# A hybrid decoder trunk on one core: the scans' row product gets another step and an explicit place in VectorE's queue

## The chip, the cores and the metric

The kernel runs on one core of one Trainium2 chip. The core has TensorE (PE, the matmuls; its weight loads are shown as PEld), VectorE (DVE), ScalarE (ACT), GpSimd (POOL) and SyncE (SP), which here only issues DMAs. Every engine works through a queue of its own, in order; semaphores tie the queues together. The metric is the device time of one execution in microseconds (us). A profile of one execution gives every instruction's start and length.

## What is computed

One inference step of two layers over 1024 prompt tokens and 8 sequences of 8 new tokens, 1088 columns in all, in fp32, model width 1024. The first layer is a Mamba-2 layer (SSD), the second a pooling layer. The change lies in the scan of the first layer. Per group of heads (8 groups, 4 heads of 64 each) and per chunk of 128 tokens, the reference does this:

```python
y_intra = jnp.einsum('bctsgr,bcsgrp->bctgrp', CB[..., None] * decay, xdt)
decay_end = jnp.exp(acum[:, :, -1:] - acum)
chunk_states = jnp.einsum('bctgn,bctgr,bctgrp->bcgrpn', B, decay_end, xdt)
chunk_decay = jnp.exp(acum[:, :, -1])
def step(h, inp):
    s, d = inp
    return d[..., None, None] * h + s, h
h_final, h_prev = lax.scan(step, h0.reshape(b, G, R, P, N), ...)
y_inter = jnp.einsum('bctgn,bctgr,bcgrpn->bctgrp', C, jnp.exp(acum), h_prev)
y = (y_intra + y_inter).reshape(b, L, H, P)
...
y = (y + d_skip.astype(jnp.float32)[:, None] * xs).reshape(b, L, D_INNER)
gated = (y * jax.nn.silu(z.astype(jnp.float32))).reshape(b, L, N_GROUPS, D_INNER // N_GROUPS)
gated = gated * lax.rsqrt(jnp.mean(gated * gated, axis=-1, keepdims=True) + EPS)
gated = gated.reshape(b, L, D_INNER) * norm_g.astype(jnp.float32)
return gated.astype(h.dtype) @ w_out, new_conv, new_ssm
```

The line before the last two, the product of the gated rows with 1/rms (and with the norm's weight), is what is moved here. It is called the row product below.

## The kernel before

Tokens lie along the columns, channels on the 128 partitions. Large matmuls are done as three passes over a split of the operands into a high and a low part (`mm3`, L190 to L192). The Mamba-2 layer runs the eight groups' scans one after the other, and beside each scan, as filling for TensorE, matmuls of something else: beside groups 0 to 4 the input projection of later groups (`proj_group`), beside groups 4 to 7 the output projection's first parts (`op_units`).

`ssd_layer` writes this interleaving out. A scan is a generator (`scan_group`) of 13 steps. Step 0 loads the first chunks' decays and does `front(0)`, step 1 `front(1)`; steps 2, 4, 6 and 8 do `states` and `rows` for two chunks and one `front`; the odd steps between do one `front`. Then the sample tokens follow. The table `FILL[g]` says how many units of filling go behind each of the first eleven steps. The last two steps of a scan are run later, out of the variable `rest`, while the next group's scan is under way:

- the first (L735 to L745) sums the squares with a matmul, takes 1/rms on ScalarE (L740 and `rstd`, L318), writes it to DRAM (`rsd`, L742) and reads it back, broadcast to all partitions (`rs`, L745). It goes behind the first unit of filling of step 0;
- the second (L748 to L758) is the row product: two VectorE instructions of 128 x 1088 (L749), each followed on SP by the store of its rows to DRAM (`gyd`, L752; not for group 7). Then the slots of `rs` and of the two row tiles are given free. It goes behind the first unit of filling of step 4, or of step 3 for groups 6 and 7. So the row product of group g - 1 is traced in group g's step.

Within a step, `states(c)` computes two chunks' states by matmuls into one PSUM tile (L615) and then the running state: for a group's first chunk a copy (L620), for every other a product on POOL (`hd`, L623) and an addition on VectorE (L624). `rows(c)` computes the two chunks' rows: the part within the chunk (L636), the part from the state (L640), and their eviction on VectorE (L607). `front(c)` transposes (L573, L576), makes the decay mask on ScalarE and VectorE (`M`, L581 to L587), the split operands (`xd`, L589), and ScalarE's copy `Bt` (L593); it also issues the load of a later chunk's decays (`acb`, L549 and L552) on SP.

A unit of `proj_group` ends in ScalarE evictions, and every third unit in a convolution on VectorE (L368 to L372). A unit of `op_units` ends in an eviction on VectorE (`op_evict`, L813, and L816 and L818 for a row's last unit) and hands its last instruction back; a unit of `proj_group` hands back nothing.

The program's order is not yet an engine's order. The instructions are first traced, in the order of the code; then a scheduler fills each engine's queue by its own estimate of when things are ready, and the code's order decides among what is ready. An instruction may so be put ahead of others that were traced before it. `self.tc.issue_after(ins)` is the means against it: whatever is traced inside its block on the engine of `ins` gets an ordering edge, and is queued behind `ins` on that engine. It adds no semaphore.

Of the kernel before, what the change touches and what calls it, by code (L numbers as in the profile page):

```python
# [11 lines left out]
ALU = mybir.AluOpType  # L12
# [87 lines left out]
class Build:  # L100
# [424 lines left out]
    def scan_group(self, g, T):  # L525
        nc, tk, gp, pp = self.nc, self.tk, self.gs, self.pp
# [83 lines left out]
        def states(c, F):  # L610

            S = pp.tile([P, 512], F32, tag="S", bufs=1, name=self.name("S"))
            for i in range(2):
                xde, Bt = F[i][3:5]
                nc.tensor.matmul(S[:, 256 * i:256 * i + 256], Bt, xde.rearrange("p r q -> p (r q)"), start=True, stop=True)  # L615
            for i in range(2):
                cd, Si = F[i][5], S[:, 256 * i:256 * i + 256]
                hn = gp.tile([P, 4, 64], F32, tag="h", bufs=3, name=self.name("h"))
                if h[-1] is None:
                    nc.vector.tensor_copy(hn.rearrange("p r q -> p (r q)"), Si)  # L620
                else:
                    hd = gp.tile([P, 4, 64], F32, tag="hd", bufs=1, name=self.name("hd"))
                    nc.gpsimd.tensor_tensor(out=hd, in0=h[-1], in1=cd.unsqueeze(2).to_broadcast([P, 4, 64]), op=ALU.mult)  # L623
                    nc.vector.tensor_tensor(out=hn, in0=hd, in1=Si.rearrange("p (r q) -> p r q", r=4), op=ALU.add)  # L624
                h.append(hn)

        def rows(c, F):

            py = [pp.tile([P, 512], F32, tag="y", bufs=2, name=self.name("y")) for _ in range(2)]
            for i in range(2):  # L630
                tok, M, xdt, _, _, _, ct = F[i]
                hc, a = h[-3 + i], 128 * i
                for q in range(2):
                    for rr in range(2):
                        r, o = 2 * q + rr, slice(64 * rr, 64 * rr + 64)
                        nc.tensor.matmul(py[q][o, a:a + 128], xdt[:, r, :], M[:, r, :], start=True, stop=(hc is None))  # L636
                    if hc is not None:
                        for rr in range(2):
                            r, o = 2 * q + rr, slice(64 * rr, 64 * rr + 64)
                            nc.tensor.matmul(py[q][o, a:a + 128], hc[:, r, :], ct[:, r, :], start=False, stop=True)  # L640
            for q in range(2):
                evac_y(py[q], q, slice(128 * c, 128 * c + 256), 256)
# [62 lines left out]
        for c in range(0, 8, 2):  # L705
            states(c, F)
            if c == 6:
                load_z()
            Fn = [front(c + 2)]
            if c == 6:  # L710
                self.slots.free(B)
            rows(c, F)
            F = Fn
            if c == 6:
                zsc = sample_inter()
                self.slots.free(C)
            yield
            if c < 6:
                F.append(front(c + 3))
                if c == 4:  # L720
                    load_h0()
                yield
# [813 lines left out]
    def ssd_layer(self):  # L1536
        nc, sl = self.nc, self.slots
        T, rest = {0: self.G[0]["out"]}, iter(())
        self.x = [None] * 8
        self.acts = [[] for _ in PARTS]  # L1540
        self.prep = self.op_part_load(0, self.acts[0])
        self.fill = self.beside(T)
        for g in range(8):
            sc = self.scan_group(g, T[g])
            for i, n in enumerate(FILL[g]):
                next(sc)
                for j in range(n):
                    next(self.fill)
                    if i in (0, 3 + (g < 6)) and j == 0:
                        next(rest, None)  # L1550
                if i == 8 and g + 1 in self.G:
                    T[g + 1] = [sl.get("xbc") for _ in range(4)]
                    for t, d in zip(T[g + 1], self.xbd[g + 1]):
                        nc.sync.dma_start(t, d)
            rest = sc
        self.prep = self.op_part_load(3, self.acts[3])
        self.out_unit()
        next(rest)
        for _ in range(2):
            next(self.fill)  # L1560
        self.out_unit()
        for _ in rest:
            pass
# [331 lines left out]
```

## Time and profile before

| | us |
|---|---|
| three runs | 1605.86, 1607.51, 1612.53 |
| median | 1607.51 |
| profiled execution | 1606.84 |
| its span | 1605.1 |
| mean granted clock of TensorE | 0.997 |

In the profile, a row of the timeline is: start, duration, engine, line, operation, result and operands by their names in the program, shapes, count; in brackets the time that the engine stood idle ahead of it and what ended that. A row of the waits is: who waited, for whom, us in total, how often, the longest. The lines are those of the kernel before. The scans lie between about 340 and 930 us; before them comes the input projection for the first groups, after them the rest of the output projection and the pooling layer. Starts in the chain of waits and in the timeline are from the span's start.

### The profile page before, as it was taken

The page shows a single profiled execution, that of the slowest core. Times are in us where ns is not written, and L with a number is a line of the kernel's source. Part 1 is how long each engine was busy: PE and PEld are TensorE (multiplying, and loading weights), DVE is VectorE, ACT ScalarE, POOL GpSimd, SP SyncE. Part 2 cuts the span into 40 slices and gives each one's busy share as a digit, 9 for nine tenths or more (in the row PEclk, how much of TensorE's full clock was granted, in tenths as well). Part 3 has the DMA queues.
Part 4 walks back from the last instruction along what each step waited for, and adds up shares of the span by engine and source line. Part 5 has one row for each costly group of instructions (what it writes and reads, how often), then busy time and mean ns, then how long its engine had stood idle before and what let it go on. Part 6 is the DMA issues. An engine that isn't in the chain of part 4 may idle for free.

```text
span 1605.1 us, 30689 instructions
## 1 busy us (share of the span) xinstructions
PE 1579.7 (98%) x11946; PEld 1506.9 (94%) x11946; DVE 1292.1 (80%) x2152; ACT 789.5 (49%) x1512; POOL 515.3 (32%) x558
## 2 busy tenths in 40 slices
PE   9999999999999999999999999999999999999997
PEld 7899999998888888888899899999999999999997
DVE  6875879778788888888888867998889867677886
ACT  6663344456666766675545437632322233333364
POOL 0133456512231313130212232265666640000241
PEclk9999999999999999999999999999999999999999
DMA  9423232355555554678998542133323379565783
GB/s 352 166 100 110 69 111 91 102 186 158 187 161 171 156 177 150 214 252 292 303 338 296 206 135 86 53 134 114 115 102 104 111 233 373 152 172 178 161 173 121
DMA packets 122306, 275.58 MB, mean 172 GB/s; under 512 B 18193, under 2 KB 59313, under 8 KB 122161
## 3 DMA queue, kind: packets, MB, share of 16 engines
q1 hardware_dynamic: 118128, 260.90, 47.7%
q0 software_dynamic: 4032, 12.72, 4.7%
q8 instruction: 94, 1.54, 0.4%
q14 instruction: 52, 0.42, 0.1%
HBM read 201.12 MB, written 70.23 MB: 169 GB/s over the span
## 4 chain that ended last, share of the span: by engine, by line
PE 81%; DVE 7%; DMA 5%; issue 4%; ACT 2%; POOL 1%; SPq 0%; DVEq 0%; ACTq 0%; POOLq 0%
PE st L1042 10%; PE st L1040 10%; PE st L1041 10%; PE mm L190 10%; PE mm L191 9%; PE mm L192 9%; PE op L1259 2%; PE op L1260 2%; PE op L1258 2%; PE y L636 2%; PE y L640 2%; DMA rsd<-z 2%; PE S L615 2%; DMA rs<-rsd 1%; PE am L261 1%
## 5 line engine op out<-in xcount | busy, mean ns | idle before, releaser
L1040 PE MATMUL st<-hh,w 128*128 128x272 f32 x832 | 240.2, 289 | 1.0 <-ACT w L182 1.0
L1042 PE MATMUL st<-hh,w 128*128 128x272 f32 x832 | 240.4, 289 | 0.4 <-DVE w L184 0.4
L1041 PE MATMUL st<-hl,w 128*128 128x272 f32 x832 | 240.0, 288 | 0.0
L1040 PE MATMUL st<-t,w 128*128 128x272 f32 x624 | 179.6, 288 | 0.0
L1042 PE MATMUL st<-t,w 128*128 128x272 f32 x624 | 179.5, 288 | 0.0
L1041 PE MATMUL st<-t,w 128*128 128x272 f32 x624 | 179.2, 287 | 0.0
L190 PE MATMUL mm<-hh,wh 128*128 128x368 f32 (+1 forms) x528 | 178.6, 338 | 0.0
L191 PE MATMUL mm<-hl,wh 128*128 128x368 f32 (+1 forms) x528 | 173.1, 328 | 0.0
L192 PE MATMUL mm<-hh,wl 128*128 128x368 f32 (+1 forms) x528 | 172.9, 327 | 0.0
L1040 PEld LDWEIGHTS st<-hh,w 128*128 128x128 f32 x832 | 156.8, 188 | 1.4 <-ACT w L182 1.4
L1042 PEld LDWEIGHTS st<-hh,w 128*128 128x128 f32 x832 | 156.4, 188 | 0.9 <-DVE w L184 0.9
L1041 PEld LDWEIGHTS st<-hl,w 128*128 128x128 f32 x832 | 156.7, 188 | 0.0
L623 POOL TENSOR_TENSOR hd<-h,cd 128x256 f32<-128x256 f32 x56 | 46.9, 838 | 313.3 <-DVE h L624 154.6
L182 ACT ACTIVATE w<-wr 128x512 fp32r<-128x512 f32 x104 | 64.9, 629 | 166.4 <-PE st L1042 135.0
L1259 PE MATMUL op<-b,w 128*128 128x272 f32 x448 | 128.9, 288 | 0.7 <-DVE b L1188 0.7
L1258 PE MATMUL op<-b,w 128*128 128x272 f32 x448 | 129.4, 289 | 0.0
L1260 PE MATMUL op<-b,w 128*128 128x272 f32 x448 | 128.9, 288 | 0.0
L190 PE MATMUL mm<-gh,wh 128*128 128x368 f32 (+1 forms) x372 | 126.0, 339 | 0.2
L192 PE MATMUL mm<-gh,wl 128*128 128x368 f32 (+1 forms) x372 | 122.1, 328 | 0.0
L191 PE MATMUL mm<-gl,wh 128*128 128x368 f32 (+1 forms) x372 | 121.8, 327 | 0.1
L1040 PEld LDWEIGHTS st<-t,w 128*128 128x128 f32 x624 | 117.7, 189 | 0.1
L1042 PEld LDWEIGHTS st<-t,w 128*128 128x128 f32 x624 | 117.4, 188 | 0.0
(307 smaller groups left out, 4572.7 us busy)
## 6 DMA issues: line engine op xcount, KB each, us to landing
wr<-win SPq DMA_DIRECT2D x48, 512.0 KB, 3.8
acb<-acd SPq DMA_DIRECT2D x64, 256.0 KB, 4.2
wr<-pin SPq DMA_DIRECT2D x32, 512.0 KB, 3.7
wr<-pout SPq DMA_DIRECT2D x28, 512.0 KB, 4.9
x<-x1d SPq DMA_DIRECT2D x24, 544.0 KB, 5.8
x1d<-x SPq DMA_DIRECT2D x22, 544.0 KB, 4.5
wr<-pout POOLq DMA_DIRECT2D x20, 512.0 KB, 6.6
x<-xT SPq DMA_DIRECT2D x16, 544.0 KB, 6.8
```

The costliest lines, as they stand in the source:

```text
L182: self.nc.scalar.activation(hi, src, AF.Copy)
L190: nc.tensor.matmul(ps[:, :n], hi[:, k, :], ah[:, a:a + n], start=first, stop=False)
L191: nc.tensor.matmul(ps[:, :n], hi[:, k, :], al[:, a:a + n], start=False, stop=False)
L192: nc.tensor.matmul(ps[:, :n], lo[:, k, :], ah[:, a:a + n], start=False, stop=last)
L615: nc.tensor.matmul(S[:, 256 * i:256 * i + 256], Bt, xde.rearrange("p r q -> p (r q)"), start=True, stop=True)
L623: nc.gpsimd.tensor_tensor(out=hd, in0=h[-1], in1=cd.unsqueeze(2).to_broadcast([P, 4, 64]), op=ALU.mult)
L1040: nc.tensor.matmul(ps[c][:, :QUART], hi[:, k], xh[:, t], start=(k == 0), stop=False)
L1041: nc.tensor.matmul(ps[c][:, :QUART], hi[:, k], xl[:, t], start=False, stop=False)
L1042: nc.tensor.matmul(ps[c][:, :QUART], lo[:, k], xh[:, t], start=False, stop=(k == 3))
L1258: nc.tensor.matmul(ps[:, :QUART], hi[:, k], xh, start=k == 0, stop=False)
L1259: nc.tensor.matmul(ps[:, :QUART], hi[:, k], xl, start=False, stop=False)
L1260: nc.tensor.matmul(ps[:, :QUART], lo[:, k], xh, start=False, stop=k == 7)
```

## The change

The row product's step is traced in step 3 for every group, where groups 1 to 5 had it in step 4. Around it stand two ordering edges: to `self.hins`, which `states` sets to its last update of the state (L620 or L624; in step 3 this is the second update of the group's first two chunks), and, where the unit of filling just run hands back an instruction (groups 5 to 7), to that instruction, the unit's last eviction. Both are on VectorE, so the edges concern the two instructions of L749. The first step of `rest` stays where it was, without an edge.

```diff
                 if h[-1] is None:
-                    nc.vector.tensor_copy(hn.rearrange("p r q -> p (r q)"), Si)
+                    ins = nc.vector.tensor_copy(hn.rearrange("p r q -> p (r q)"), Si)
                 else:
...
-                    nc.vector.tensor_tensor(out=hn, in0=hd, in1=Si.rearrange("p (r q) -> p r q", r=4), op=ALU.add)
+                    ins = nc.vector.tensor_tensor(out=hn, in0=hd, in1=Si.rearrange("p (r q) -> p r q", r=4), op=ALU.add)
                 h.append(hn)
+            self.hins = ins.ins
...
                 for j in range(n):
-                    next(self.fill)
-                    if i in (0, 3 + (g < 6)) and j == 0:
+                    ins = next(self.fill)
+                    if i == 0 and j == 0:
                         next(rest, None)
+                    elif i == 3 and j == 0:
+                        with self.tc.issue_after(self.hins), self.tc.issue_after(ins.ins) if ins else contextlib.nullcontext():
+                            next(rest, None)
```

## The prediction

> **What bounds the kernel now.** I read the page first, for the share of each engine.
>
> ```profile
> PE 1579.7 (98%) x11946; PEld 1506.9 (94%) x11946; DVE 1292.1 (80%) x2152; ACT 789.5 (49%) x1512; POOL 515.3 (32%) x558
> ```
>
> TensorE is busy for 98% of the span, so an edit of VectorE's queue can only gain where TensorE waits. Next I read the waits of TensorE between 340 and 960 us, the part of the span that holds the scans (columns: us in total, times, longest).
>
> ```profile
> PE y L640 <- DVE h L620: 4.1, 4, 1.2
> PE S L615 <- ACT Bt L593: 2.2, 2, 1.4
> PE mm L796 <- ACT raw L434: 2.0, 1, 2.0
> PE y L636 <- DVE M L587: 1.5, 1, 1.5
> ```
>
> The waits of TensorE there add up to 4.1 + 2.2 + 2.0 + 1.5 = 9.8 us (one more, of 0.3, is left out). The largest is that of the inter-chunk row matmul (L640) for the first copy of the state (L620), four times, about 1 us each. Why the copy is late shows in the answer for the row product's line (L749): until what VectorE stood idle ahead of it, in us and times. The chain of waits (start, duration, what) adds where that DMA comes from.
>
> ```profile
>   DMA rs<-rsd: 9.9, 6
> ```
>
> ```profile
> 428.49 5.61 DMA rsd<-z
> 434.12 3.84 DMA rs<-rsd
> ...
> 449.97 0.59 PE y L640 x8
> ...
> 661.20 1.35 DVE xbc L749
> ```
>
> The product of the group before stands ahead of the copy in VectorE's queue, and waits there until the broadcast of 1/rms has come back from DRAM. VectorE stands still for 9.9 us in six such waits, though only four of them reach TensorE. The chain holds such a product four times, first at 437.99 and last at 661.20, so these are groups 1 to 4 (the copy of the group that runs, behind the product of the one before).
>
> **Groups 1 to 4: the wait that goes.** VectorE in the second group (start, duration, line; in brackets the idle time and what ended it), and the state's matmul that the copy needs:
>
> ```profile
> 437.99 1.35 DVE L749 SCALAR_TENSOR_TENSOR xbc<-xbc,vec,rs 128x1088 f32<-128x1088 f32 x1 [2.16 <-DMA rs<-rsd]
> 439.25 0.42 DVE L620 COPY h<-S 128x256 f32<-128x256 f32 x1
> ...
> 448.87 0.41 DVE L624 TENSOR_TENSOR h<-hd,S 128x256 f32<-128x256 f32 x1
> ...
> 454.33 1.34 DVE L749 SCALAR_TENSOR_TENSOR xbc<-xbc,vec,rs 128x1088 f32<-128x1088 f32 x1
> ```
>
> ```profile
> 435.82 0.70 PE L615 MATMUL S<-xd,Bt 128*128 128x256 f32 x2
> ...
> 439.73 0.66 PE L640 MATMUL y<-ea,h 128*64 128x128 f32 x8 [1.19 <-DVE h L620]
> ```
>
> The edge to the state's last update puts both products behind the copy. VectorE is free from 437.99 - 2.16 = 435.83 on and the state's matmul ends at 435.82 + 0.70 = 436.52, so the copy moves from 439.25 to about 436.5, 2.7 us earlier. The row matmul could have begun at 439.73 - 1.19 = 438.54, and the copy is done by then (436.94), with 1.6 us to spare. That takes away 1.19 us here and 4.1 us in the four groups. The broadcast lands at 437.96 and no longer blocks anything, since the next thing that VectorE does is the copy.
>
> By the Trainium skill, "Perfetto Trace Analysis", section "Identifying the Most-Contended Engine", the busy share of matmuls is a poor measure of the headroom and that of the weight loads a better one. The trace has this row for the weight loads:
>
> ```profile
> PEld y L640 <- DVE h L620: 4.9, 4, 1.4
> ```
>
> By it the sum below would come out 4.9 - 4.1 = 0.8 us lower. The trace before doesn't say which of the two rows counts; the rest of this text goes by the matmuls.
>
> **What the products cost where they go.** Nothing is added or dropped: 16 products of 1.35 us, as before, and no DMA more. In groups 1 to 4 the step moves from 4 to 3. The trace tells where that puts them: the second product, traced in step 4, now runs at 454.33, behind that step's updates; so products traced in step 3 will run ahead of step 4's first update (now at 448.87), both of them, 1.35 + 1.34 = 2.69 us. From the copy to that update VectorE has 448.87 - 439.25 = 9.62 us. With the copy at 436.52 the update comes at 436.52 + 9.62 + 2.69 = 448.83 and ends at 449.25. Its reader is the row matmul at 449.97, which by then has moved to 449.97 - 1.19 = 448.78: a new wait of 0.47 us, four times 1.9 us. If one of the products or none falls ahead of the update, this is nothing; that is the lower bound, and I take the upper, because of the row at 454.33. The 2.7 us that the copy gains can be lost on the way too, where its followers wait for TensorE or ScalarE, which don't move with it: then the wait is up to 2.69 us in each group, which is the slower rival below.
>
> **The stores behind the product.** SP's queue is in order too. Two of its rows, one of ScalarE's, and the page's row for the loads (size, us from issue to landing):
>
> ```profile
> 439.36 0.32 SPq L752 DMA_DIRECT2D gyd<-xbc  x1
> 439.78 5.33 SPq L549 DMA_DIRECT2D acb<-acd  x2
> ```
>
> ```profile
> 447.97 1.27 ACT L581 ACTIVATE M<-acb,tka 128x128 f32<-128x128 f32 x4
> ```
>
> ```profile
> acb<-acd SPq DMA_DIRECT2D x64, 256.0 KB, 4.2
> ```
>
> The store of the product (L752) waits on SP for the product, and the load of a chunk's decays stands right behind it. If that order stays and the first product runs at about 444, the load starts some 5 us later. It takes 4.2 us, so it lands now at 444.0 and would land at about 449. By the count of its tiles its reader is the last instruction of the row at 447.97 (about 448.9). So this is covered to within a few tenths; without the cover ScalarE would stand still for up to 5 us in each of four groups. I take 0.
>
> **Groups 5 to 7: the edge to the eviction.** Here the fill is the output projection and both products must also follow one eviction (L818 or L813). For groups 5 and 6 these are the eviction and the next update on VectorE and the update's reader on TensorE:
>
> ```profile
> 750.04 0.22 DVE L818 TENSOR_TENSOR x<-x,gs 128x64 f32<-128x64 f32 x1
> ...
> 752.81 0.42 DVE L624 TENSOR_TENSOR h<-hd,S 128x256 f32<-128x256 f32 x1 [0.49 <-issue]
> 754.07 0.66 PE L640 MATMUL y<-ea,h 128*64 128x128 f32 x8
> ```
>
> ```profile
> 818.66 0.22 DVE L818 TENSOR_TENSOR x<-x,gs 128x64 f32<-128x64 f32 x1
> ...
> 819.61 0.42 DVE L624 TENSOR_TENSOR h<-hd,S 128x256 f32<-128x256 f32 x1 [0.21 <-issue]
> 821.13 0.39 PE L640 MATMUL y<-ea,h 128*64 128x128 f32 x4
> ```
>
> In group 5 the update ends at 753.23, 0.84 us before its reader; in group 6 at 820.03, 1.10 us before it. Both products move from ahead of the eviction to behind it, so VectorE reaches the eviction up to 2.69 us earlier and spends these 2.69 us after it: nothing if the eviction can follow, at most 2.69 - 0.84 = 1.85 and 2.69 - 1.10 = 1.59 us if it can't. I take 0 for both: VectorE shows no idle time ahead of either eviction, so the eviction was waiting for VectorE and can come earlier.
>
> Group 7, VectorE and then TensorE:
>
> ```profile
> 879.28 1.35 DVE L749 SCALAR_TENSOR_TENSOR xbc<-xbc,vec,rs 128x1088 f32<-128x1088 f32 x1 [1.46 <-DMA rs<-rsd]
> ...
> 884.28 0.59 DVE L813 SCALAR_TENSOR_TENSOR x<-mm,gat,x 128x368 f32<-128x368 f32 x1
> ```
>
> ```profile
> 884.19 0.70 PE L615 MATMUL S<-xd,Bt 128*128 128x256 f32 x2 [1.36 <-ACT Bt L593]
> ...
> 886.52 0.44 PE L640 MATMUL y<-ea,h 128*64 128x128 f32 x4
> ```
>
> Here VectorE's wait (1.46) and the first product are what make the split operands of chunk 3 late, and with them ScalarE's copy Bt and TensorE's 1.36 us. With both products behind 884.28 that wait goes: -1.36. VectorE reaches the eviction up to 1.46 + 1.35 = 2.81 us earlier, and not before TensorE has done the unit, whose last matmul stands just ahead of the state's (884.19 - 1.36 = 882.83). I put it at 882.5 to 882.8, estimated from that row; with its 0.59, the products' 2.69 and the update's 0.42 the update ends at about 886.3; its reader moves to 886.52 - 1.36 = 885.16 and waits about 1.0 us. Net about -0.4, between -1.4 (no new wait) and 0.
>
> **The sum.** -4.1 + 1.9 - 0.4 = -2.6 us, between -4.1 - 1.4 = -5.5 and -4.1 + 1.9 + 1.85 + 1.59 = +1.2. The profiled execution took 1606.84 (span 1605.1), so it would take 1604.2. The median of the three runs shown, 1607.51, is 0.67 above it; from there it is 1604.9, which is my forecast. Its own range is 1602 to 1608.7.
>
> **Rivals.**
>
> The next wait takes its place, nothing is gained. The copy is early, but the row matmul's other inputs or the POOL product between the updates end last instead. Against it: the 1.6 us to spare. For it: the updates behind the copy still need POOL's product (hd) between them. About 1607.
>
> More goes than the four waits. VectorE's 9.9 us of standing still are out of the queue; if its lead also covers ScalarE's Bt copies and the masks (2.2 and 1.5 us of TensorE's waits) and the hand-over of group 4 (2.0), 9.8 us go: 1607.51 - 9.8 = 1597.7. Against it: only the 4.1 and 1.36 stand directly behind a product.
>
> Slower: two products in a row become the bound. They are one block of 2.69 us behind the update, on an engine that is busy for 80% of the span. If nothing covers the block, the next mask, split or update is 2.69 us late in seven groups: 18.8 us, less the 5.5 that go, +13.3: 1620.8. It turns slower from 5.5 / 7 = 0.8 us uncovered per group, and by over 0.5% from about 1.9. Against it: before, VectorE carried the same block in two pieces. For it: in groups 5 to 7 the eviction's edge forbids the gaps that were used.
>
> The change doing nothing is excluded for groups 1 to 4, where a product stands ahead of the copy; in groups 6 and 7 both already stand behind the updates, and only the eviction's edge acts.
>
> **How the numbers follow.** Forecast 0.48, nothing gained 0.12, more goes 0.22, slower 0.18. Something over 0.5%, 8.0 us, is about what a measurement of this kernel can tell from no change. The first two cases lie within it: 0.60. The third is faster, 0.22, and the fourth slower, 0.18. The range runs from 1596 (all waits gone, and the 1.6 us by which the lowest run shown lies under the median) to 1613 (the slower case half covered: halfway between 1604.9 and 1620.8).
>
> **What would show it.** After: no wait of L640 for L620, and L749 without idle time before it in groups 1 to 4; L620 within some tenths of the end of its state's matmul (L615); both products between L620 and the next L624; new waits of L640 for L624 of about half a us; S waiting for Bt no longer in group 7. I am wrong if L749 still waits for its DMA, if the waits of L640 for L624 exceed 1 us per group, if M or xd become releasers of TensorE, or if loads of acb show up as releasers of ScalarE.

## The result, and the profile after

| | before | changed kernel |
|---|---|---|
| median of 6 runs, us | 1607.8 | 1602.82 |
| lowest to highest | 1605.86 to 1612.53 | 1600.84 to 1603.68 |
| profiled execution | 1606.84 | 1600.84 |
| its span | 1605.1 | 1599.0 |

The ratio is 0.997, with a 95% interval from 0.9956 to 0.9983: 2.7 to 7.1 us less than before, and no change by the bound of 0.5%. Run again beside the kernels of the experiments (a0 below), the same program gave 0.9987 [0.9979, 0.9996], or 0.6 to 3.4 us less. The two intervals share 2.7 to 3.4 us. The changed kernel's median is the same both times (1602.82 and 1602.94); it is the kernel before that came out slower in its six runs here (1607.8) than in 110 later ones on four chips (medians 1605.94 to 1606.45). So the gain is about 3 us rather than 5.

The kernel's file has one line more from L620 on, so what was L640 is L641 now, L749 is L750, and L813 is L814. The page's row of busy times:

```profile
PE 1579.0 (99%) x11946; PEld 1505.4 (94%) x11946; DVE 1293.0 (81%) x2152; ACT 789.9 (49%) x1512; POOL 515.6 (32%) x558
```

The engines do the same work as before; TensorE's 1579 us now fill a span that is 6 us shorter. TensorE's waits between 340 and 960 us (total, times, longest):

```profile
PE mm L797 <- ACT raw L434: 1.3, 1, 1.3
PE mm L190 <- DVE x L814: 1.1, 1, 1.1
PE y L641 <- DVE h L624: 0.5, 1, 0.5
PE y L637 <- DVE M L587: 0.5, 1, 0.5
...
PE S L615 <- ACT Bt L593: 0.2, 1, 0.2
...
```

The row that led the list before, 4.1 us of the row matmul waiting for the copy of the state (L620), is gone. So is the row of 2.2 us of S waiting for Bt, but for 0.2. Two waits are new: 1.1 us of a filling matmul for an eviction of the output projection (L814), and 0.5 us of the row matmul for an update of the state (L624), in group 6. Three rows of 0.2 to 0.3 us are left out. And what the row product's own line says:

```profile
L750 DVE SCALAR_TENSOR_TENSOR xbc<-xbc,vec,rs x16: 1344/1347/1355, 442.9 to 924.6; 128x1088 f32<-128x1088 f32 x16
its engine sat idle before it (us, times) until:
```

Nothing stands below the heading of the idle time, where 9.9 us for the broadcast of 1/rms stood. VectorE in the second group, and then TensorE there:

```profile
435.87 0.42 DVE L620 COPY h<-S 128x256 f32<-128x256 f32 x1 [0.33 <-PE S L615]
...
442.94 1.35 DVE L750 SCALAR_TENSOR_TENSOR xbc<-xbc,vec,rs 128x1088 f32<-128x1088 f32 x1
...
445.49 1.35 DVE L750 SCALAR_TENSOR_TENSOR xbc<-xbc,vec,rs 128x1088 f32<-128x1088 f32 x1
...
448.04 0.42 DVE L624 TENSOR_TENSOR h<-hd,S 128x256 f32<-128x256 f32 x1
```

```profile
435.13 0.70 PE L615 MATMUL S<-xd,Bt 128*128 128x256 f32 x2
...
436.92 0.66 PE L641 MATMUL y<-ea,h 128*64 128x128 f32 x8
...
449.35 0.66 PE L641 MATMUL y<-ea,h 128*64 128x128 f32 x8
```

The copy follows its matmul at once, and its reader runs without a wait. Both products stand ahead of step 4's first update. But that update's reader (449.35) doesn't wait either, 0.9 us after the update's end.

Where the 6 us went is read by stretches, cut at the starts of a group's first gated row on VectorE (L733, now L734): from group 0's to group 3's, to group 4's, and to group 7's. Before and after (stretch, length, busy time of each engine, granted clock, DMA):

```profile
420.40:643.64 223.24, 220.33 (x1710) 196.87 (x1709) 187.91 (x287) 144.74 (x327) 55.00 (x93) 1.00 0.53 170
643.64:723.27 79.63, 76.43 (x571) 69.40 (x571) 66.69 (x100) 54.77 (x116) 19.52 (x33) 0.98 0.71 231
723.27:917.86 194.59, 191.93 (x1474) 175.56 (x1473) 170.80 (x328) 99.12 (x235) 40.33 (x46) 1.00 0.84 289
```

```profile
419.75:639.41 219.66, 219.66 (x1709) 197.05 (x1708) 188.11 (x286) 144.93 (x327) 56.76 (x93) 1.00 0.54 173
639.41:717.61 78.20, 76.71 (x581) 69.29 (x580) 66.40 (x100) 54.44 (x116) 21.43 (x33) 1.00 0.71 236
717.61:911.41 193.80, 191.78 (x1465) 174.25 (x1464) 171.30 (x328) 99.58 (x235) 39.93 (x46) 1.00 0.83 290
```

In the first stretch, which holds the second to fourth groups' scans, TensorE is now busy for 219.66 of 219.66 us, and 223.24 - 219.66 = 3.58 us are gone. In the next, group 4 and its hand-over to the output projection, 1.43 are gone, and in groups 5 to 7 0.79. That is 5.8 us; the first stretch begins 0.65 us earlier in this execution, which isn't the change's doing (in a0 it begins at 420.57).

Not all of the 5.8 us is the change's doing either. The second stretch before has a granted clock of 0.98. At its end, from 719.2 us on, TensorE ran at half its clock for about 3 us, with its matmuls 0.31 us apart and not 0.167. A window of the kernel before (columns as above), and two of its matmuls:

```profile
720.00:722.00 2.00, 2.00 (x10) 2.00 (x8) 2.00 (x2) 1.84 (x4) 1.18 (x2) 0.50 1.00 384
```

```profile
720.43 0.51 PE L796 MATMUL mm<-gh,wh 128*128 128x368 f32 x1
720.73 0.51 PE L797 MATMUL mm<-gh,wl 128*128 128x368 f32 x1
```

By the clock of such windows this dip is worth some 1.7 us, an estimate. The changed kernel's stretches have none, in this execution and in a0. In a0 the three stretches are 3.52, 0.46 and 0.62 us shorter than before. So the first stretch is what both executions show; with the dip taken off, the other two together lie between 0.5 us less and 0.6 us more than before.

### The profile page after: what moved, and what is told of

It reads as the page before. It is cut to its first block, busy times and chain, and to the rows that moved or that the text cites. A ratio compares the mean times of both kernels' runs of the same rounds, so it can differ in the third digit from the quotient of the medians.

```text
span 1599.0 us, 30692 instructions
## 1 busy us (share of the span) xinstructions
PE 1579.0 (99%) x11946; PEld 1505.4 (94%) x11946; DVE 1293.0 (81%) x2152; ACT 789.9 (49%) x1512; POOL 515.6 (32%) x558
```

## The experiments

The theory after the result: (1) the gain is the product at the head of VectorE's queue, which waited for 1/rms and held the copy back; (2) the ordering edge removes it, not the step; (3) the new wait of 1.9 us that the prediction counted fell away because TensorE's queue was sorted anew too. The rivals: the step does it, groups 5 to 7 do it, or the products never come near the reader. Each kernel below keeps the line numbers of before (L749, L640, L813), and its time stands beside the kernel before on the same chip. Medians are of 9 to 12 runs each.

**e2 and e1: the step alone, and the edge to the state's update.** Against the kernel before; e2 has the first change of this diff alone, e1 has the edge too (to `self.hins`, set in `states` as in the changed kernel):

```diff
-                    if i in (0, 3 + (g < 6)) and j == 0:
+                    if i in (0, 3) and j == 0:
-                        next(rest, None)
+                        with self.tc.issue_after(self.hins) if i else contextlib.nullcontext(): next(rest, None)
```

> The row product is traced in step 3 for every group, but without either ordering edge. Theory (what counts is that the first product, which waits for its DMA, no longer stands ahead of the state's copy): without the edge the scheduler puts the first product ahead of the copy again, L640 still waits for L620 four times, about 4 us in all, and the time is that of the kernel before within 2 us (ratio 0.999 to 1.001). Rival (the earlier step alone sorts the queues better): the waits of L640 for L620 are gone and the ratio is about 0.997.

> As the changed kernel, but with the edge to the state's update alone, none to the eviction. Groups 1 to 4 are as in the changed kernel. Theory: the gain of groups 1 to 4 stays (4 to 5 us), group 7 keeps its wait for the DMA in front of the product and TensorE its wait of S for Bt (1.4 us), while the new wait of 1.1 us of TensorE for an eviction in group 5 goes: ratio 0.997 to 0.998. Rival (the eviction's edge carries a part of the gain in groups 5 to 7): 2 us or more slower than the changed kernel, ratio 0.9985 or more.

e2: 1605.27 us, ratio 0.9995 [0.9983, 1.0007]. TensorE's wait between 340 and 960 us, and from the product's line the idle time ahead of it:

```profile
PE y L640 <- DVE h L620: 3.1, 5, 1.2
```

```profile
  DMA rs<-rsd: 9.9, 6
```

e1: 1603.49 us, ratio 0.9983 [0.9974, 0.9992]. Its waits show no L640 for L620; S waits for Bt as before:

```profile
PE S L615 <- ACT Bt L593: 2.2, 3, 0.9
```

```profile
  DMA rs<-rsd: 0.9, 1
```

Without an edge the product is back at the queue's head, with all of its 9.9 us, although it was traced a step earlier: the step alone doesn't take that wait away, and the time can't be told from that of before. It isn't without effect on TensorE, though: up to group 3's first gated row the waits for the copy fall from 2.9 to 1.5 us and the stretch from 223.24 to 221.56 us, while group 5 has a wait of 1.2 us that it didn't have. With the edge no wait for the copy is left in groups 1 to 4, and the stretch is 219.70 us (e1); with the old step and the edges it is 220.18 (e3 below). Most of it is the edge. e1's ratio lies just above the range expected, which held 4 to 5 us.

**e4 and e5: which groups.** e4 has the change for groups 1 to 4, e5 for groups 5 to 7; the other groups are as before.

> The change for groups 1 to 4 alone; groups 5 to 7 have the step and the order of the kernel before. Theory: nearly all of the gain is here, 4 to 5 us, ratio 0.997 to 0.9975; L640 no longer waits for L620. Rival (groups 5 to 7 give a good part): a gain of 2.5 us or less, ratio 0.9985 or more.

> The change for groups 5 to 7 alone; groups 1 to 4 have the step and the order of the kernel before. Theory: the wait of S for Bt in group 7 goes (1.4 us), a wait for an eviction in group 5 comes (1.1 us), the four waits of L640 for L620 stay: within 1.5 us of the kernel before, ratio 0.999 to 1.001. Rival (these groups give a good part): a gain of 2.5 us or more, ratio 0.9985 or less.

e4: 1603.39 us, ratio 0.9979 [0.997, 0.9988]. e5: 1607.45 us, ratio 1.0003 [0.9993, 1.0013], with four waits of L640 for L620 left (2.7 us). The change in groups 1 to 4 gives about 3 us, less than the 4 to 5 expected; alone in groups 5 to 7 it gives nothing that can be told from zero.

**a0: the changed kernel once more**, with the line numbers of before.

> The changed kernel again, with the line numbers of before, beside the kernels it is to be compared with. All theories: about 1603 us, ratio 0.996 to 0.998 to the kernel before; TensorE shows no wait of the step-4 reader (L640) for the state's copy (L620) in any group, and the row product (L749) no idle time before it.

1602.94 us, ratio 0.9987 [0.9979, 0.9996]; the kernel before took 1605.98 on this chip. The ratio lies just above the range expected, the waits are as expected. Its first stretch:

```profile
420.57:640.29 219.72, 219.72 (x1710) 197.17 (x1708) 187.62 (x286) 144.85 (x327) 56.62 (x93) 1.00 0.53 173
```

219.72 against 219.66: the period of a group is 73.2 us in both executions.

**e7: the reader held in its place.** In TensorE's queue, the reader of step 4's first update stood behind 12 matmuls of filling before the change. In the changed kernel it stands behind 20, some 0.167 us each (counted in TensorE's timeline of the second group, from the L636 ahead of them on). e7 is the changed kernel with edges on TensorE that keep all but 12 of them behind that reader, by putting the unit's later matmuls (`k > 3`), the small matmuls (L261) traced behind the unit, and step 5's `front` and unit behind it (the diff shows a part of this):

```diff
-                            nc.tensor.matmul(py[q][o, a:a + 128], hc[:, r, :], ct[:, r, :], start=False, stop=True)
+                            self.yins = nc.tensor.matmul(py[q][o, a:a + 128], hc[:, r, :], ct[:, r, :], start=False, stop=True)
...
-            self.mm1(ps, w, k, act, ch, k == 0, k == len(acts) - 1)
+            with self.tc.issue_after(self.pin.ins) if self.pin and k > 3 else contextlib.nullcontext(): self.mm1(ps, w, k, act, ch, k == 0, k == len(acts) - 1)
...
-                next(sc)
+                with self.tc.issue_after(self.yins.ins) if i == 5 and 0 < g < 5 else contextlib.nullcontext(): next(sc)
```

> The changed kernel, with edges on TensorE in groups 1 to 4 so that step 4's first reader of the state (L640) stands behind 12 matmuls of filling, as before the change, and not behind 20. Theory A (the prediction's term of 1.9 us was right for a queue of TensorE that stays as it was, and fell away because it was sorted anew): four waits of L640 for L624 of about 0.45 us each, 1.5 to 2.5 us in all, and 1604 to 1606 us, some 1 to 2 us above the changed kernel. Rival B (the products never reach the reader wherever it stands): no such wait, and the time of the changed kernel within 0.7 us. Rival C (a wait appears and is absorbed later, since the scan's eight matmuls have filling behind them that isn't tied to them): the waits as in A, the time as in B.

1606.43 us, ratio 1.0 [0.999, 1.001], beside a0's 0.9987: 0.0013, or 2.1 us, and 3.5 us by the medians. TensorE's waits from the first gated row of group 0 (419.84) to that of group 4 (720.4), and one of the readers:

```profile
PE y L640 <- DVE h L624: 1.7, 4, 0.4
```

```profile
448.64 0.66 PE L640 MATMUL y<-ea,h 128*64 128x128 f32 x8 [0.44 <-DVE h L624]
```

Four waits of about 0.44 us, where the prediction had 0.47. The first stretch shows that they aren't absorbed later:

```profile
419.84:641.53 221.69, 220.39 (x1710) 197.15 (x1709) 187.89 (x286) 144.94 (x327) 56.70 (x93) 1.00 0.54 172
```

221.69 - 219.72 = 1.97 us in three groups, 0.66 in each. Theory A holds: the new wait is there as soon as the reader is left where it was. With it nothing is left of the gain, since the ratio is 1.0; the median lies 0.4 us above theory A's range. What the rival C had for it, filling that isn't tied to the reader, doesn't help an engine that works its queue in order and has no gap later on.

**e3, e9 and e10: both edges, with the step of before.** In a0's form only the step's number differs: 4 for groups 1 to 5 (e3), for groups 1 to 4 (e9), for group 5 (e10).

```diff
-                    if i in (0, 3) and j == 0:
+                    if i in (0, 3 + (g < 6)) and j == 0:
```

> Both edges (behind the state's update and behind the last eviction), but the product traced in step 4 for groups 1 to 5 as before. Theory A (the place in VectorE's queue alone is what counts, and the edges alone set it): the same as the changed kernel, 1602 to 1604 us, no wait of L640 for L620 and no idle time before L749. Theory B (the step counts as well, because a step brings its own units of filling): the products come behind step 4's first update, step 5's update waits for them instead, and the time lies at 1604 to 1607 us.

e3: 1607.28 us, ratio 1.0011 [1.0003, 1.002]: 4.3 us above a0 and slower than the kernel before, and yet without one wait of L640 for L620 and with no idle time ahead of L749. Theory A of this run falls, and so does B: no update waits, and the group's period is 73.36 us, 0.14 above a0's. What is lost, is lost in group 7, and the two halves show from where:

> Both edges everywhere, the product traced in step 4 in groups 1 to 4 only. In the run with the old step everywhere, a group's period was 73.36 us against 73.22 in the changed kernel, and group 7's time between the gated rows of chunk pairs (L733) 60.7 against 54.2. Theory A (in groups 1 to 4 the step hardly counts, since the edge sets the queue's order; the loss of 4 us comes from group 5's step alone, whose store moves the loads of the decays for group 7): 1603 to 1604 us, the period 73.36 us, at most 0.6 us above the changed kernel. Rival B (the step counts in groups 1 to 4 too, in some way that the periods don't show): 1605 us or more.

> Both edges everywhere, the product traced in step 4 in group 5 only. Theory A: three loads of decays (acb) of group 7 issued some 12 us later on SP (at about 863 rather than 851), ScalarE behind, TensorE waiting for the copy Bt about 2 us in group 7, and 1606 to 1608 us, about 4 us above the changed kernel. Rival B: the changed kernel's time within 1 us.

e9: 1602.35 us, ratio 0.9976 [0.9967, 0.9986]. e10: 1607.01 us, ratio 1.001 [1.0001, 1.0019]. The stretch between the first gated rows of groups 6 and 7, of a0 and then of e10:

```profile
859.22:913.43 54.21, 54.15 (x426) 49.14 (x425) 48.80 (x99) 29.63 (x74) 12.78 (x16) 1.00 0.73 260
```

```profile
857.21:917.93 60.72, 57.95 (x431) 49.85 (x430) 49.64 (x99) 31.81 (x82) 13.57 (x16) 1.00 0.74 247
```

It is 6.5 us longer, while the stretch of groups 5 and 6 is 1.4 us shorter. The matmuls (first column) stand still in it for 60.72 - 57.95 = 2.8 us rather than for nothing, the weight loads (second) for 60.72 - 49.85 = 10.9 rather than 54.21 - 49.14 = 5.1. So 5.8 of the 6.5 us show as missing weight loads, and only half of that as idle matmuls. The trace points to SP's queue, of a0 and then of e10:

```profile
850.79 1.85 SPq L549 DMA_DIRECT2D acb<-acd  x3
```

```profile
860.85 0.32 SPq L1627 DMA_DIRECT2D x1d<-x  x1
861.22 2.48 SPq L549 DMA_DIRECT2D acb<-acd  x3
```

Three loads of group 7's decays are queued behind a store that waits for an eviction until 860.85. ScalarE in e10, which has its masks to make from them:

```profile
862.24 0.28 ACT L593 ACTIVATE Bt<-tr 128x128 f32<-128x128 f32 x1 [4.83 <-DVE xd L589]
...
866.79 1.28 ACT L581 ACTIVATE M<-acb,tka 128x128 f32<-128x128 f32 x4 [2.01 <-DMA acb<-acd]
```

In a0 ScalarE made these masks from 856.11 on. In e10 it does so 10.7 us later and is behind from there on; TensorE then waits for Bt:

```profile
PE S L615 <- ACT Bt L593: 2.4, 3, 1.6
```

So in groups 1 to 4 the step makes no difference that can be told, and in group 5 it decides over some 4 us, which are lost two groups later. That the loads of the decays are the cause is read from the trace; moving them alone, and why the queues are sorted so, wasn't tried.

**e6: the product ahead of the copy, with and without its wait.** Both kernels put both products of groups 1 to 4 ahead of the copy (behind the mask of chunk 1, L587, in step 1). In the second, the rows of groups 0 to 3 are multiplied by themselves and not by 1/rms, which leaves the normalisation of these groups out and takes the wait for the reload away. The orders of VectorE's and TensorE's queues are the same in both.

```diff
-                                           in1=rst,
+                                           in1=rst if g > 3 else xs[q],
```

> For groups 1 to 4 the row product is traced in step 1, so that both products stand ahead of the state's copy (L620) in VectorE's queue; the queue's head then waits for the reload of 1/rms with the copy behind it. Theory A (what costs is a product at the head of the queue whose row is still under way, with the copy behind it): the copy comes about 4 us later than in the changed kernel, TensorE's reader L640 waits about 2 to 3 us for it in each of four groups, 1607 to 1613 us, 4 to 10 us above its twin without the reload. Rival B (the products' own busy time ahead of the copy costs, not the wait for the reload): both twins the same within 1 us, and both above the changed kernel by 3 us or more. Rival C (the place in the queue costs nothing): both at 1602 to 1604 us.

> As its twin, but for groups 0 to 3 the rows are multiplied by themselves rather than by the reloaded 1/rms, which leaves the normalisation of these groups out and takes the wait for the reload away; the queues of VectorE and TensorE are the same in both. Theory A: the two products run at once, the copy comes about 2.7 us after the point at which the first could start, TensorE's reader L640 waits 0 to 0.5 us for it, 1602 to 1605 us. Rival B: the time of its twin within 1 us.

With the reload: 1607.76 us, ratio 1.0012 [1.0003, 1.002]; without: 1605.12 us, ratio 1.0 [0.9989, 1.0011]. TensorE's waits between 340 and 960 us of the first, and VectorE at its second group; then VectorE of the second kernel at the same place:

```profile
PE y L640 <- DVE h L620: 3.7, 4, 1.8
```

```profile
437.81 2.61 DVE L749 SCALAR_TENSOR_TENSOR xbc<-xbc,vec,rs 128x1088 f32<-128x1088 f32 x2 [1.78 <-DMA rs<-rsd]
440.34 0.42 DVE L620 COPY h<-S 128x256 f32<-128x256 f32 x1
```

```profile
438.28 2.61 DVE L749 SCALAR_TENSOR_TENSOR xbc<-xbc,vec 128x1088 f32<-128x1088 f32 x2
440.81 0.42 DVE L620 COPY h<-S 128x256 f32<-128x256 f32 x1
```

In the second the wait of L640 for L620 is gone altogether. So with the same queues the reload at their head costs 2.6 us by the medians, and 3.7 us show as TensorE's waits: theory A in kind. Its size was off, 3.7 us rather than 8 to 12; the copy's reader too was queued later, behind 11 matmuls of filling. Rival B holds in part: without the wait the time is still that of the kernel before (ratio 1.0), 1.7 us above e4 (on another chip), whose groups 5 to 7 are as here. From group 0's first gated row to group 3's the two take 223.14 and 220.72 us, and e4 219.71. So of 3.4 us lost there, 2.4 go with the wait and 1.0 with the place of the products ahead of the copy. That 1.0 us shows in no wait of TensorE's matmuls, and where it arises is open.

**e8: groups 5 and 6 as before**, the change for groups 1 to 4 and 7.

> The change for groups 1 to 4 and 7; groups 5 and 6 as before. Theory A (the change's gain lies in the queue-head wait of groups 1 to 4 and in group 7's wait for Bt, and group 5 lost about 1.1 us to an eviction that comes late for a feed-forward matmul): 0.5 to 1.5 us under the changed kernel, 1601.5 to 1602.5 us, a wait of L640 for L620 of about 1.0 us once (group 5), no wait of S for Bt in group 7. Rival B (groups 5 and 6 are a wash, the one wait traded for the other): the changed kernel's time within 0.5 us.

1602.85 us, ratio 0.9982 [0.9973, 0.999], as a0 within the intervals. The new wait for the eviction was gone but for 0.2 us, group 5 had a wait of 0.8 for the copy (before, it had none), and in group 7 S waited for Bt again, in another chunk:

```profile
889.37 0.70 PE L615 MATMUL S<-xd,Bt 128*128 128x256 f32 x2 [1.59 <-ACT Bt L593]
```

Rival B holds. None of these versions can be told from the changed kernel to its advantage; e9's median is the lowest, by 0.6 us on another chip than a0's.

## Why the prediction came out as it did

The forecast was 1604.9 us and 2.6 us of gain; measured were 1602.8 and 5.0, and 2 to 3 us in the repeat. The time lies in the range and within 0.5% of before, as the likeliest case had it. That 2.6 lies so near the repeat is luck in part: without the term that failed the sum would have been -4.5, and waits that it took at nothing came up in groups 5 and 6. By its steps:

- **The wait that goes, -4.1: right.** The copy was put at the end of its matmul; that ends at 435.13 + 0.70 = 435.83, and the copy came at 435.87. No such wait is left, and e2 against e1 shows that the edge does it. The size was rather above: three groups' periods lost 3.58 us, where the rows of the matmuls had 1.2 + 0.8 + 0.9 = 2.9 for these groups. The weight loads' rows had 1.4 + 1.0 + 1.1 = 3.5. In e7 likewise: 1.97 us in three groups, by the matmuls' rows 1.3, by those of the weight loads 2.2. The rule of the Trainium skill, "Perfetto Trace Analysis", section "Identifying the Most-Contended Engine", that the prediction set beside its sum, speaks of busy shares and not of single waits. Carried over to waits, as the prediction did, it agrees with these traces better than the matmuls' rows do: its 0.8 us belonged into the sum.
- **The new wait in groups 1 to 4, +1.9: the step that failed**, at the words "its reader is the row matmul at 449.97, which by then has moved to 449.97 - 1.19 = 448.78". VectorE's side of it was exact: the update was put at 448.83, and came at 448.04 in an execution whose group began 0.65 to 0.7 us earlier. The reader was not left where it was: with 20 matmuls of filling ahead of it, not 12, it came at 449.35, and the prediction's place for it in this execution would have been about 448.1. That is the 8 x 0.167 = 1.3 us more. e7 puts it back, and the wait of 0.44 us appears four times. The term was right for an unchanged queue of TensorE; the change re-sorted that queue as well. (449.97 is the reader's start in the chain. The timeline has it at 449.90, and by it the term is 0.54 us for each group.)
- **Group 7, -1.4 + 1.0: half right.** The eviction and the products follow each other as put, and S waits no more. The new wait didn't come; by the rows the reader stands later here too, though no run held this one in its place. VectorE and then TensorE in group 7:

```profile
878.20 0.60 DVE L814 SCALAR_TENSOR_TENSOR x<-mm,gat,x 128x368 f32<-128x368 f32 x1
878.72 2.60 DVE L750 SCALAR_TENSOR_TENSOR xbc<-xbc,vec,rs 128x1088 f32<-128x1088 f32 x2
881.24 0.42 DVE L624 TENSOR_TENSOR h<-hd,S 128x256 f32<-128x256 f32 x1
```

```profile
878.00 1.02 PE L615 MATMUL S<-xd,Bt 128*128 128x256 f32 x4
...
881.97 0.66 PE L641 MATMUL y<-ea,h 128*64 128x128 f32 x8
```

  The update ends 881.66 - 878.00 = 3.66 us after S begins (put at 886.3 - 882.83 = 3.5), the reader runs 3.97 us after it and not 2.33. Alone, without the changed groups before, it is worth nothing that can be told (e5), and in e8 its wait came back elsewhere.
- **Groups 5 and 6, taken at 0: too little, but within the bounds.** Group 6 has a wait of 0.5 us for the update (0.8 in a0), where the bound was 1.59. At the end of group 5 there is one for an eviction, which the prediction did not have. The changed kernel, and then e1, which lacks only the edge to the eviction:

```profile
790.49 0.43 PE L190 MATMUL mm<-gh,wh 128*128 128x368 f32 x1 [1.06 <-DVE x L814]
```

```profile
792.58 0.43 PE L190 MATMUL mm<-gh,wh 128*128 128x368 f32 x1 [0.22 <-DVE x L813]
```

  At this place it is 0.7 to 1.1 us in all seven versions that have the edge to the eviction in groups 5 and 6 (the changed kernel, a0, e3, e5, e7, e9, e10), and at most 0.3 in all the others; the 1.4 us that e2 has for an eviction stand elsewhere, at 730.70. So it comes with that edge; by which way isn't shown. What went away in group 7 outweighs it: the stretch of groups 5 to 7 got 0.8 us shorter all the same (0.6 in a0).
- **The stores on SP, taken at 0: right, and for another reason than given.** The two loads of decays (L549) that stood right behind the first store now stand ahead of both stores, at 437.54 and 442.95. A load that does stand behind a store (L552, at 447.07) is issued 1.9 us earlier than before, where it came at 448.97. SP after:

```profile
442.95 0.37 SPq L549 DMA_DIRECT2D acb<-acd  x1
444.31 0.32 SPq L753 DMA_DIRECT2D gyd<-xbc  x1
447.07 0.37 SPq L552 DMA_DIRECT2D acb<-acd  x1
447.53 0.46 SPq L753 DMA_DIRECT2D gyd<-xbc  x1
```

  The concern itself was sound: e3 and e10, where loads of the decays come 10 us late, are about 4 us slower. But loads of acb as releasers of ScalarE were no sign to go by: between 340 and 960 us ScalarE waits for them 29.3 us in all before, and 25.2 after.
- **The slower rival** needed 0.8 us of the products' block uncovered in each of seven groups. e7, with the reader in its old place, has 0.66 in groups 1 to 4, and that alone takes the gain away. It was nearer than its reasons against made it look.

What is open: why TensorE's queue is sorted as it is, on which the missing new wait rests, and by which way the edge to the eviction brings the wait at the end of group 5.

## What to carry to other kernels

An instruction that waits for a DMA doesn't belong ahead of one that TensorE needs, even if nobody needs its own result soon; an ordering edge on its engine moves it, while tracing it earlier left it at the queue's head (e2). But where a scheduler sorts the queues, an edge on one engine re-sorts the others too, so that a term of the form "this moves, its reader stays" needs the new order of the reader's queue, or both ends in the range. One step's difference in group 5 cost as much as the whole change brought, so a variant is judged by the whole time and not by the wait that it was made for. And two single profiles can differ by a dip of the clock: 6.0 us lay between the two profiled executions here, and about 3 us between the kernels.

## What the runs showed of the hardware

A wait of TensorE costs more than the idle time that the matmul's row shows, by 0.1 to 0.2 us each time. Four pairs, each with three waits between the first gated rows of groups 0 and 3, show it: what the stretch lost, against the rows of the one wait that differs (L640 for the state), by the matmuls and by the weight loads.

| | lost, us | matmuls | weight loads |
|---|---|---|---|
| before, against the changed kernel | 3.58 | 2.9 | 3.5 |
| e7, against a0 | 1.97 | 1.3 | 2.2 |
| e2, against e1 | 1.86 | 1.5 | 2.1 |
| e6 with the reload, against its twin | 2.42 | 1.9 | 2.8 |

The weight loads are the nearer measure in all four, within 0.4 us. The two rows of e7, in its first stretch (419.84 to 641.53):

```profile
PE y L640 <- DVE h L624: 1.3, 3, 0.4
...
PEld y L640 <- DVE h L624: 2.2, 3, 0.7
```

The granted clock of TensorE dips now and then within an execution. Seven of the fourteen profiles have one dip each between 340 and 960 us (before, e1, e2, e3, e5 and both of e6), the others none. By windows of 4 us each dip is worth 1.6 to 1.7 us, as that from 719.2 us on in the kernel before, with a clock of 0.50 in its middle.
